# Three raw tiles of gated activations instead of four in the down stage of a decoder layer's MLP

## The chip, the cores and the metric

The kernel runs on one core of a Trainium2 chip. The metric is the device time of one execution in microseconds (us). TensorE does the matmuls, VectorE (DVE), ScalarE (ACT) and GpSimd (POOL) the elementwise work, and SyncE (SP) issues nearly all transfers between main memory and the on-chip memory, in the order of its queue.

## The reference

One layer of a hybrid decoder, float32, 2048 tokens of width 1024: a mixer of three head groups, then a gated MLP of 2688 channels, each with a residual. Only the MLP and the last norm matter here:

```python
h = rmsnorm(x, norm_ffn[l])
gate = causal_dwconv(h @ ffn_w_gate[l], ffn_conv_w[l], ffn_conv_b[l])   # width 3, along time
x = x + (jax.nn.gelu(gate) * (h @ ffn_w_val[l])) @ ffn_w_down[l]
...
return rmsnorm(x, norm_final)
```

## The kernel before, in words

Matrices are multiplied in split form: a float32 operand becomes a high half (a copy rounded to the matmul's type, made by ScalarE, line L100) and a low half (the rest, made by VectorE, L107), and `mm3` issues three matmuls for each product (L130 to L132). The helper `split` makes both halves; `load_w` loads a block of weights into a tile "wr" and splits it into "wh" and "wl".

The MLP goes over the tokens in two halves of 1024 (`hf` 0 and 1). In each half an *up stage* (`up`) goes over the NFF = 21 blocks of 128 channels; I call them channels 0 to 20. It makes the gate gr, its convolution and GELU ga, and the value v, from matmuls that all stand on line L993; its last steps are an add into gr (L1010), an add into v (L1013), another into gr (L1015), two convolution steps into ga (L1022), the GELU, the product v (L1025), and the store of v to main memory, `g_ffn[f]` (L1026). The tiles gr, ga and v of even channels, so of channel 20, lie in the pool f_up0, those of odd channels, so of channel 19, in f_up1.

The *down stage* (`down`) then multiplies g_ffn by w_down. It goes over groups of 2 to 4 row blocks of 128 tokens (3, 3 and 2 in the first half, 4 and 4 in the second). A group has 21 steps, one for each channel block: load a block of w_down, load the group's columns of g_ffn[f] into a raw tile "graw" (L1054), split that into "gh" and "gl", and issue 6 matmuls for each row block. In the first half a step is 18 matmuls with three row blocks and 12 with two. The next half's input is prepared beside the first half's down stage (tiles xt, L137 to L151, and the transposes).

```python
graw = gp.tile([P, 4 * P], F32, name="graw", bufs=4)[:, :n * P]
sync.dma_start(out=graw, in_=g_ffn[f][:, t0 * P:(t0 + n) * P])
g = [gp.tile([P, 4 * P], F32R, name=nm, bufs=3)[:, :n * P] for nm in ("gh", "gl")]
with tc.high_priority(offset=160):
    split(graw, g[0], g[1])
```

The up and down stages use the same memory, one after the other. In bytes of one partition from its start, the up stage leaves 8,192 free, then come channel 19's tiles in f_up1 (gr from 8,192), then channel 20's in f_up0: gr from 20,512, ga, v. The down stage's area f_g starts at 320 and holds graw, gh and gl in tiles of 2,048 bytes, with 4, 3 and 3 of them, so it ends at 320 + 10 x 2,048 = 20,800; its last tile is the gl of step 1. The area f_o with the norm's weights nfb and the residuals xr follows it. A down tile waits only for those up tiles whose bytes it takes (`reuse_waits="tile"`).

The order of instructions on each engine is made when the program is built, by a scheduler that places an instruction once it takes it to be ready, by priority; `tc.high_priority` moves an instruction forward. At run time each engine and the SP queue go through their own order and stop at an instruction whose inputs or tiles are not there.

Of the kernel before, what the change touches and what calls it, by code (L numbers as in the profile page):

```python
# [8 lines left out]
F32 = mybir.dt.float32  # L9
# [7 lines left out]
P = 128  # L17
# [26 lines left out]
def kernel(ctx: ExitStack, tc: tile.TileContext, x, norm_mix, w_in, hgrn_lower_bounds, hgrn_norm,  # L44
# [10 lines left out]
    def pool_at(stack, nbytes, name, bufs, **kw):  # L55

        stack.enter_context(tc.tile_pool(name="pad_" + name, bufs=1, **kw)).tile([P, nbytes // 4], F32, name="pad")
        return stack.enter_context(tc.tile_pool(name=name, bufs=bufs, **kw))
# [21 lines left out]
    def mm_bank():  # L80
        return bank("mm", 4)

    def aux_bank():
        return bank("aux", 2)

    def sc_bank():
        return bank("sc", 2)
# [16 lines left out]
    def split(raw, hi, lo, e_hi=act, e_lo=vec):  # L104

        copy(e_hi, hi, raw)
        e_lo.tensor_tensor(lo, raw, hi.bitcast(F32), op=ALU.subtract)  # L107

    def load_w(src, n1, n2, tag, tail=None, wpool=None, wcols=D):

        def part(pool_, dt, nm):
            return pool_.tile([P, wcols], dt, name=nm, tag=nm)[:, :n1 * n2].rearrange("p (a b) -> p a b", b=n2)
        hl = [part(wpool or wsp, F32R, "wh"), part(wpool or wsp, F32R, "wl")]
        raw = part(wraw, F32, "wr")
        if tail is None:
            sync.dma_start(out=raw, in_=src)
        else:
            m = src.shape[-1]
            sync.dma_start(out=raw[:, :, :m], in_=src)
            sync.dma_start(out=raw[:, :, m:], in_=tail)  # L120
        e_hi, e_lo, ahead = W_SPLIT[tag]
        with tc.high_priority(offset=ahead):
            split(raw, hl[0], hl[1], getattr(nc, e_hi), getattr(nc, e_lo))
        return hl
# [3 lines left out]
    def mm3(o, lhs, rhs, first, last):  # L128
        (lh, ll), (rh, rl) = lhs, rhs
        pe.matmul(o, lh, rh, start=first, stop=False)  # L130
        pe.matmul(o, lh, rl, start=False, stop=False)  # L131
        pe.matmul(o, ll, rh, start=False, stop=last)  # L132
# [90 lines left out]
    with ExitStack() as cx:  # L223
# [328 lines left out]
        for gi, group in enumerate((rows, frows)):  # L552
            n = sum(r[2] for r in group)
# [86 lines left out]
        for b in LEVELS[:5]:  # L640
            n = 64 // b
# [67 lines left out]
    with ExitStack() as cy:  # L709
# [319 lines left out]
        def down(hf, groups, gp, op, nfb, beside=()):  # L1029

            beside, t0, nst = list(beside), hf * TH // P, sum(1 for _ in groups) * NFF
            every, cnt = (nst // (len(beside) + 1) if beside else nst), 0
            for gi, n in enumerate(groups):
                banks = [[aux_bank(), sc_bank()] if t < 2 else [mm_bank(), mm_bank()] for t in range(n)]
                xr, ops = [], []

                def residuals():
                    for t in range(n):
                        two = n > 3 and t > 1
                        xr.append(xpool.tile([P, D], F32, name="xr2", tag="xt") if two else  # L1040
                                  op.tile([P, D], F32, name="xr", bufs=3))
                        r0 = (t0 + t) * P
                        sync.dma_start(out=xr[t], in_=x2_d[r0 // TB][r0 % TB:r0 % TB + P, :])

                def mms(t, h, f):
                    g, wd = ops[f]
                    mm3(banks[t][h], [a[:, t * P:(t + 1) * P] for a in g], [a[:, h, :] for a in wd],
                        f == 0, f == NFF - 1)

                late = 3 if (hf, gi) == (NH2 - 1, len(groups) - 1) else 2  # L1050
                for f in range(NFF):
                    wd = load_w(w_down[f * P:(f + 1) * P, :].rearrange("p (a c) -> p a c", a=2), 2, 512, "ffd")
                    graw = gp.tile([P, 4 * P], F32, name="graw", bufs=4)[:, :n * P]
                    sync.dma_start(out=graw, in_=g_ffn[f][:, t0 * P:(t0 + n) * P])  # L1054
                    g = [gp.tile([P, 4 * P], F32R, name=nm, bufs=3)[:, :n * P] for nm in ("gh", "gl")]
                    with tc.high_priority(offset=160):
                        split(graw, g[0], g[1])
                    ops.append((g, wd))
                    if f < NFF - late:
                        for t in range(n):  # L1060
                            for h in range(2):
                                mms(t, h, f)
                    if f == 8:
                        if gi == 0:
                            sync.dma_start(out=nfb, in_=norm_final.partition_broadcast(P))
                        residuals()
                    cnt += 1
                    if beside and cnt % every == 0:
                        beside.pop(0)()
                for t in range(n):  # L1070
                    y, sq = xr[t], op.tile([P, 2], F32, name="sq2", bufs=4)
                    for h in range(2):
                        for f in range(NFF - late, NFF):
                            mms(t, h, f)
                        ysl = y[:, h * 512:(h + 1) * 512]
                        vec.tensor_tensor(ysl, banks[t][h], ysl, op=ALU.add)
                        act.activation(junk_t(), ysl, AF.Square, accum_out=sq[:, h:h + 1])  # L1077
                    r = small.tile([P, 1], F32, name="rstd")
                    vec.tensor_tensor(r, sq[:, 0:1], sq[:, 1:2], op=ALU.add)
                    vec.tensor_scalar(r, r, 1.0 / D, EPS, op0=ALU.mult, op1=ALU.add)  # L1080
                    pool.tensor_tensor(r, r, half, op=ALU.pow)  # L1081
                    for h in range(2):
                        ysl = y[:, h * 512:(h + 1) * 512]
                        vec.scalar_tensor_tensor(ysl, ysl, r, nfb[:, h * 512:(h + 1) * 512], op0=ALU.mult, op1=ALU.mult)  # L1084
                        sync.dma_start(out=out[(t0 + t) * P:(t0 + t + 1) * P, h * 512:(h + 1) * 512], in_=ysl)
                t0 += n
            for st in beside:
                st()
# [5 lines left out]
        for hf in range(NH2):  # L1094
            with ExitStack() as cu:
                upools = [pool_at(cu, 8192, "f_up1", 1, reuse_waits="tile")]
                upools.insert(0, cu.enter_context(tc.tile_pool(name="f_up0", bufs=1, reuse_waits="tile")))
                up(hf, H, upools)
            with ExitStack() as cd_:
                gp = pool_at(cd_, 320, "f_g", 3, reuse_waits="tile")  # L1100
                op = cd_.enter_context(tc.tile_pool(name="f_o", bufs=1, reuse_waits="tile"))
                nfb = op.tile([P, D], F32, name="nfb")
                if hf + 1 < NH2:
                    H, steps = h_steps(hf + 1)
                    down(hf, (3, 3, 2), gp, op, nfb, steps)
                else:
                    down(hf, (4, 4), gp, op, nfb)
# [30 lines left out]
```

## Time and profile before

| | |
|---|---|
| median of 3 runs | 2282.15 us (2281.91 to 2282.93) |
| the profiled execution | 2290.03 us, with a span of 2288.3 us from first to last instruction |
| mean granted TensorE clock | 0.986 |
| first half: up stage, down stage | to 1381 us, to about 1630 us |
| second half: up stage, down stage | to 2036 us, to 2288 us |

Times in the rows are microseconds from the start of the profiled execution's span. A matmul's duration overlaps with the next one's, so distances between starts are used. The granted clock is the share of full speed at which TensorE was let run.

### The profile page before, as it was taken

To read this page: it belongs to the slowest core of one execution; us is meant where nothing else is said; L and a number is where in the kernel's file an instruction comes from. 1 tells how busy PE (TensorE), PEld (TensorE's weight loads), DVE (VectorE), ACT (ScalarE), POOL (GpSimd) and SP (SyncE) were. 2 spreads that over 40 slices of the span, in tenths; PEclk is the share of its full clock that TensorE was granted. 3 is DMA by queue.
4 is the path that set the end of the run, shared out by engine and by line. 5 is a ranking of instruction groups with operands and counts; after the bars stand their busy time and mean duration, and the time that the engine had idled before them with its cause. 6 is when DMAs were issued, how large, how long until landed. Compare 5 with 4: busy or idle time off the path is not lost. (4 is left out here: it accounts for less than half of the span.)

```text
span 2288.3 us, 31745 instructions
## 1 busy us (share of the span) xinstructions
PE 2195.2 (96%) x12310; PEld 1806.5 (79%) x12310; DVE 1591.1 (70%) x2212; ACT 998.1 (44%) x1375; POOL 350.3 (15%) x456
## 2 busy tenths in 40 slices
PE   7999999998999999999999998999999999989998
PEld 6887777776668789888888886888788888868886
DVE  7799998989577777766666664667766666643534
ACT  4453535342175375544444443556444444433322
POOL 2231432325242410000000000000000000000000
PEclk9999999999899999999999999999999999989999
DMA  7443322355146555622222236676522222254552
GB/s 260 130 148 115 136 80 61 93 174 176 28 143 222 164 167 170 205 85 83 83 83 83 84 101 199 191 240 227 175 83 83 83 83 83 83 172 150 173 181 88
DMA packets 272980, 307.27 MB, mean 134 GB/s; under 512 B 17203, under 2 KB 226110, under 8 KB 271294
## 3 DMA queue, kind: packets, MB, share of 16 engines
q1 hardware_dynamic: 272830, 305.26, 42.1%
q8 instruction: 96, 1.57, 0.3%
q14 instruction: 54, 0.44, 0.1%
HBM read 243.34 MB, written 61.87 MB: 133 GB/s over the span
## 5 line engine op out<-in xcount | busy, mean ns | idle before, releaser
L107 DVE TENSOR_TENSOR wl<-wr,wh 128x1024 fp32r<-128x1024 f32 (+2 forms) x289 | 328.3, 1139 | 130.8 <-ACT wh L100 125.9
L100 ACT ACTIVATE wh<-wr 128x1024 fp32r<-128x1024 f32 (+3 forms) x265 | 257.4, 974 | 251.4 <-PE mm L993 76.3
L130 PE MATMUL mm<-hTh,wh 128*128 128x512 f32 x576 | 235.0, 408 | 0.0
L132 PE MATMUL mm<-hTh,wl 128*128 128x512 f32 x576 | 232.6, 404 | 1.5 <-POOL wl L107 1.1
L131 PE MATMUL mm<-hTl,wh 128*128 128x512 f32 x576 | 233.1, 405 | 0.0
L398 POOL TENSOR_TENSOR qc<-Q,X 32x128 f32<-32x128 f32 x224 | 151.0, 674 | 247.2 <-ACT X L384 120.3
L107 DVE TENSOR_TENSOR gl<-graw,gh 128x384 fp32r<-128x384 f32 (+2 forms) x105 | 60.8, 583 | 183.3 <-ACT gh L100 173.9
L100 ACT ACTIVATE wh<-s 128x1024 fp32r<-128x1024 f32 x84 | 89.2, 1062 | 199.8 <-PE sc L993 173.2
L100 ACT ACTIVATE gh<-graw 128x384 fp32r<-128x384 f32 (+2 forms) x105 | 56.8, 544 | 240.1 <-PE mm L131 194.0
L131 PE MATMUL sc<-wl,oh 128*128 128x256 f32 x512 | 147.7, 289 | 2.2 <-DVE wl L107 2.2
L130 PE MATMUL sc<-wh,oh 128*128 128x256 f32 x512 | 147.2, 289 | 1.4 <-DVE xr L828 1.4
L132 PE MATMUL sc<-wh,ol 128*128 128x256 f32 x512 | 146.0, 285 | 0.0
L132 PEld LDWEIGHTS mm<-hTh,wl 128*128 128x128 f32 x576 | 109.1, 189 | 30.0 <-issue 4.3
L130 PEld LDWEIGHTS mm<-hTh,wh 128*128 128x128 f32 x576 | 109.2, 190 | 29.1 <-issue 7.1
L131 PEld LDWEIGHTS mm<-hTl,wh 128*128 128x128 f32 x576 | 109.1, 189 | 28.1 <-issue 7.3
L993 PE MATMUL mm<-t34h,wh 128*128 128x512 f32 x336 | 130.8, 389 | 0.0
L993 PE MATMUL mm<-t34l,wh 128*128 128x512 f32 x336 | 130.7, 389 | 0.0
L993 PE MATMUL mm<-t34h,wl 128*128 128x512 f32 x336 | 130.7, 389 | 0.0
L107 DVE TENSOR_TENSOR wl<-s,wh 128x1024 fp32r<-128x1024 f32 x84 | 102.5, 1221 | 9.5 <-ACT wh L100 9.5
L1022 DVE SCALAR_TENSOR_TENSOR ga<-gr,pcol,ga 128x1024 f32<-128x1024 f32 x84 | 107.7, 1282 | 0.1
L130 PE MATMUL aux<-wh,gh 128*128 128x512 f32 x210 | 83.6, 398 | 21.7 <-ACT gh L100 21.7
L131 PEld LDWEIGHTS sc<-wl,oh 128*128 128x128 f32 x512 | 98.2, 192 | 5.8 <-DVE wl L107 2.9
(302 smaller groups left out, 5696.0 us busy)
## 6 DMA issues: line engine op xcount, KB each, us to landing
wr<-in_ffn_w_down_dram SPq DMA_DIRECT2D x105, 512.0 KB
wr<-in_w_in_dram SPq DMA_DIRECT2D x80, 512.0 KB
wr<-in_ffn_w_gate_dram SPq DMA_DIRECT2D x42, 512.0 KB
wr<-in_ffn_w_val_dram SPq DMA_DIRECT2D x42, 512.0 KB
g_ffn<-v SPq DMA_DIRECT2D x42, 512.0 KB
wr<-in_w_out_dram SPq DMA_DIRECT2D x32, 512.0 KB
graw<-g_ffn SPq DMA_DIRECT2D x42, 256.0 KB
xt<-in_x_dram SPq DMA_DIRECT2D x16, 512.0 KB
```

The lines of the kernel that those rows point to most:

```text
L100: act.activation(o, i, AF.Copy)
L107: e_lo.tensor_tensor(lo, raw, hi.bitcast(F32), op=ALU.subtract)
L130: pe.matmul(o, lh, rh, start=first, stop=False)
L131: pe.matmul(o, lh, rl, start=False, stop=False)
L132: pe.matmul(o, ll, rh, start=False, stop=last)
L398: pool.tensor_tensor(qc[p_, h, :].rearrange("p (n s) -> p n s", s=lev), qo[p_, 2], xo[p_, 2], op=ALU.mult)
L993: pe.matmul(o, lhs[a], rhs[b], start=first and k == 0 and i == 0, stop=k == KH - 1 and i == 2, skip_group_check=True)
L1022: vec.scalar_tensor_tensor(ga, gr[:, k:k + TH], pc[f"fw{k}"][:, f:f + 1], ga, op0=ALU.mult, op1=ALU.add)
```

## The change

One number: the raw tiles of gated activations are three instead of four. f_g then ends at 320 + 9 x 2,048 = 18,752, below byte 20,512 where channel 20's gr starts, and f_o starts 2,048 bytes lower.

```diff
-                    graw = gp.tile([P, 4 * P], F32, name="graw", bufs=4)[:, :n * P]
+                    graw = gp.tile([P, 4 * P], F32, name="graw", bufs=3)[:, :n * P]
```

TensorE's order is the same as before. SP's changes at the start of the first down stage; below, g_ffn_97 to g_ffn_117 are the blocks of channels 0 to 20, x_d is the residual's stream in main memory, and "wr" a block of w_down. Before:

```order
L1026 DMA g_ffn_116<-v 128x1024
L116 DMA wr<-in_ffn_w_down_dram 128x1024 x4
L1026 DMA g_ffn_117<-v 128x1024
L1054 DMA graw<-g_ffn_97 128x384
L1054 DMA graw<-g_ffn_98 128x384
L1054 DMA graw<-g_ffn_99 128x384
L1054 DMA graw<-g_ffn_100 128x384
L1065 DMA nfb<-in_norm_final_dram 128x1024
```

And now, from the same store of channel 19:

```order
L1026 DMA g_ffn_116<-v 128x1024
L1054 DMA graw<-g_ffn_97 128x384
L1054 DMA graw<-g_ffn_98 128x384
L1054 DMA graw<-g_ffn_99 128x384
L116 DMA wr<-in_ffn_w_down_dram 128x1024
L1054 DMA graw<-g_ffn_100 128x384
L116 DMA wr<-in_ffn_w_down_dram 128x1024
L1054 DMA graw<-g_ffn_101 128x384
L1054 DMA graw<-g_ffn_102 128x384
L116 DMA wr<-in_ffn_w_down_dram 128x1024 x2
L1026 DMA g_ffn_117<-v 128x1024
```

The first loads of graw moved from behind the store of channel 20 to right behind that of channel 19, ahead of four loads of w_down. At the start of the second down stage SP's order changes in the same way, except that one load of w_down stands between the second and the third graw.

On VectorE, in the last channel of the first up stage, before:

```order
L107 TENSOR_TENSOR wl<-wr,wh 128x512
L1010 TENSOR_TENSOR gr<-aux,gr 128x512
L107 TENSOR_TENSOR wl<-wr,wh 128x1024
L1013 TENSOR_TENSOR v<-mm,v 128x512
L1015 TENSOR_TENSOR gr<-sc,gr 128x512
L107 TENSOR_TENSOR wl<-wr,wh 128x1024
L1022 SCALAR_TENSOR_TENSOR ga<-gr,pcol_400,ga 128x1024 x2
L107 TENSOR_TENSOR wl<-wr,wh 128x1024
L1025 TENSOR_TENSOR v<-ga,v 128x1024
L107 TENSOR_TENSOR gl<-graw,gh 128x384 x4
```

And now:

```order
L107 TENSOR_TENSOR wl<-wr,wh 128x512
L107 TENSOR_TENSOR gl<-graw,gh 128x384
L1010 TENSOR_TENSOR gr<-aux,gr 128x512
L107 TENSOR_TENSOR wl<-wr,wh 128x1024
L107 TENSOR_TENSOR gl<-graw,gh 128x384 x2
L1013 TENSOR_TENSOR v<-mm,v 128x512
L1015 TENSOR_TENSOR gr<-sc,gr 128x512
L107 TENSOR_TENSOR wl<-wr,wh 128x1024
L1022 SCALAR_TENSOR_TENSOR ga<-gr,pcol_400,ga 128x1024 x2
L107 TENSOR_TENSOR wl<-wr,wh 128x1024
L1025 TENSOR_TENSOR v<-ga,v 128x1024
L107 TENSOR_TENSOR gl<-graw,gh 128x384
```

Three low halves "gl" moved from behind the product v of channel 20 to places between its adds. ScalarE's high halves moved with them. In the second half the third stands behind the add into v (L1013).

The third place is SP's queue at the start of the two-block group, around the stores of the group before it ("out"), as a piece of the difference:

```order
 L1054 DMA graw<-g_ffn_100 128x256
-L116 DMA wr<-in_ffn_w_down_dram 128x1024
-L1054 DMA graw<-g_ffn_101 128x256
 L116 DMA wr<-in_ffn_w_down_dram 128x1024
 L1085 DMA out_dram<-xr 128x512 x2
 L1043 DMA xr<-x_d_119 128x1024
 L1085 DMA out_dram<-xr 128x512
-L116 DMA wr<-in_ffn_w_down_dram 128x1024 x2
+L116 DMA wr<-in_ffn_w_down_dram 128x1024
+L1054 DMA graw<-g_ffn_101 128x256
+L116 DMA wr<-in_ffn_w_down_dram 128x1024
```

The load for step 4 (g_ffn_101) moved from ahead of three stores to behind them. Elsewhere in the down stages a load of graw stands one step later than before in the same way.

## Rows read from the trace of the kernel before

**Rows 1.** The page, busy time, share of the span and instructions of an engine.

```profile
PE 2195.2 (96%) x12310; PEld 1806.5 (79%) x12310; DVE 1591.1 (70%) x2212; ACT 998.1 (44%) x1375; POOL 350.3 (15%) x456
```

**Rows 2.** TensorE's waits, 1375 to 1720 us, then 2035 to the end.

```profile
PE aux L130 <- ACT gh L100: 10.5, 1, 10.5
PE sc L993 <- DVE wl L107: 1.2, 1, 1.2
...
PE aux L130 <- ACT gh L100: 11.3, 1, 11.3
```

**Rows 3.** Busy time by stretch around the first seam, with clock and data share.

```profile
core 0: us, PE busy (x) PEld busy (x) DVE busy (x) ACT busy (x) POOL busy (x), PEclk, DMA share, GB/s
1360.00:1380.00 20.00, 20.00 (x90) 16.57 (x89) 13.69 (x16) 11.27 (x16) 1.46 (x4) 1.00 0.39 131
1380.00:1390.00 10.00, 1.16 (x6) 0.62 (x4) 5.41 (x5) 3.05 (x4) 0.00 (x0) 0.83 0.62 188
1390.00:1400.00 10.00, 8.37 (x26) 6.74 (x27) 2.36 (x5) 2.94 (x5) 0.00 (x0) 0.66 0.89 293
1400.00:1410.00 10.00, 10.00 (x45) 8.26 (x45) 4.50 (x5) 2.96 (x4) 0.00 (x0) 1.00 0.62 189
```

**Rows 4.** The SP queue in order of time: start, duration, instruction, count.

```profile
1361.61 4.05 SPq L145 DMA_DIRECT2D xt<-x_d  x2
1366.55 0.32 SPq L1026 DMA_DIRECT2D g_ffn<-v  x1
...
1385.47 0.33 SPq L1026 DMA_DIRECT2D g_ffn<-v  x1
1385.85 0.42 SPq L1054 DMA_DIRECT2D graw<-g_ffn  x1
```

**Rows 5.** First seam, order of time; in brackets the idle time before.

```profile
1380.77 0.39 PE L993 MATMUL mm<-t34h,wl 128*128 128x512 f32 x1
...
1391.06 1.46 ACT L100 ACTIVATE gh<-graw 128x384 fp32r<-128x384 f32 x3 [6.87 <-DMA graw<-g_ffn]
...
1391.63 0.79 PE L130 MATMUL aux<-wh,gh 128*128 128x512 f32 x1 [10.47 <-ACT gh L100]
...
1396.84 0.40 PE L130 MATMUL mm<-wh,gh 128*128 128x512 f32 x1
...
1401.62 0.39 PE L130 MATMUL mm<-wh,gh 128*128 128x512 f32 x1
```

**Rows 6.** Second seam, order of time.

```profile
2036.06 0.39 PE L993 MATMUL mm<-t34h,wl 128*128 128x512 f32 x1
...
2041.21 2.44 SPq L1054 DMA_DIRECT2D graw<-g_ffn  x4
...
2047.04 0.63 ACT L100 ACTIVATE gh<-graw 128x512 fp32r<-128x512 f32 x1 [7.50 <-DMA graw<-g_ffn]
...
2047.73 0.79 PE L130 MATMUL aux<-wh,gh 128*128 128x512 f32 x1 [11.27 <-ACT gh L100]
...
2052.37 0.39 PE L132 MATMUL sc<-wh,gl 128*128 128x512 f32 x1
```

**Rows 7.** VectorE and TensorE in the last channel before the first seam.

```profile
1375.76 0.69 DVE L1013 TENSOR_TENSOR v<-mm,v 128x512 f32<-128x512 f32 x1 [0.62 <-PE mm L993]
...
1378.28 0.39 PE L993 MATMUL mm<-t34h,wh 128*128 128x512 f32 x1
...
1383.01 1.22 DVE L107 TENSOR_TENSOR wl<-wr,wh 128x1024 fp32r<-128x1024 f32 x1
```

**Rows 8.** Start of the two-block group, order of time.

```profile
1578.25 0.42 DVE L107 TENSOR_TENSOR gl<-graw,gh 128x256 fp32r<-128x256 f32 x1
...
1581.06 0.41 DVE L107 TENSOR_TENSOR gl<-graw,gh 128x256 fp32r<-128x256 f32 x1
...
1581.60 0.38 SPq L1054 DMA_DIRECT2D graw<-g_ffn  x1
...
1585.68 0.42 ACT L100 ACTIVATE gh<-graw 128x256 fp32r<-128x256 f32 x1 [0.74 <-DMA graw<-g_ffn]
1585.85 0.39 PE L132 MATMUL aux<-wh,gl 128*128 128x512 f32 x1
```

## The prediction

> **What bounds the kernel now.** I read the page first: TensorE is busy for 96% of the span [rows 1]. So only the other 4% can be had, and the question is where they lie and whether the change touches one of them. TensorE's waits in the two down stages answer it [rows 2]: one wait of 10.5 and one of 11.3 us, each at the start of a down stage, both for a high half "gh" of the gated activations, which ScalarE makes; the next longest is 1.2 us. The busy times by stretch show the first hole from the clock's side [rows 3]: from 1380 to 1390 us TensorE works 1.16 us of 10, in the next 10 us its granted clock is 0.66, and from 1400 us on the clock is full and there is no gap.
>
> Then the rows around that hole, in order of time. The SP queue stores channel 19 at 1366.55, channel 20 at 1385.47, and only behind that store, at 1385.85, issues the first load "graw" [rows 4]. TensorE's last matmul of the up stage had started at 1380.77; ScalarE splits the load at 1391.06, and TensorE goes on at 1391.63 [rows 5]. So the hole is a store that waits for the last gate's arithmetic, then a load queued behind it that needs nothing from it (it reads what channel 0 stored), then 5.2 us of landing (1385.85 to 1391.06), then the split. The second hole is alike, with 5.8 us of landing (2041.21 to 2047.04) [rows 6].
>
> **The change part by part.** No instruction is added or removed; some move, as the orders above show. Three loads now stand directly behind the store of channel 19, about 19 us earlier in the first down stage, and on VectorE the first three low halves stand between the steps of channel 20's gate instead of behind it. The code says why: with four tiles the area f_g ran to byte 20,800, past the start (20,512) of the last channel's gr; with three it ends at 18,752.
>
> *Removed, first hole.* At full clock a matmul of the down stage starts every (1401.62 - 1396.84) / 21 = 0.2276 us [rows 5]. The next one could have started at 1380.77 + 0.23 = 1381.00 and started at 1391.63: 10.63 us. The 12 matmuls from there to 1396.84 took 5.21 us instead of 12 x 0.2276 = 2.73, the clock being at the lower of its two levels (1.2 of 2.4 GHz) after the hole: 2.48 us.
>
> *Removed, second hole.* From 2036.06 + 0.23 = 2036.29 to 2047.73: 11.44 us. The 11 matmuls from there to 2052.37 took 4.64 us instead of 2.50: 2.14 us [rows 6]. The four terms make **26.7 us**.
>
> *What is late next.* Step k of the first down stage (18 matmuls, 4.10 us) would start at 1381.00 + 4.10 k and needs block k of w_down split. Of the first three blocks the last split began at 1383.01 and took 1.22 us [rows 7], for a step that starts at 1389.2. Blocks 3 to 5 were asked for ahead of the store of 1385.47, as the queue's order shows, and block 3 is needed at 1393.3. Nothing is late; I cost this at zero.
>
> *Added ahead of the up stage's end.* Three splits, about 0.5 us each on ScalarE (1.46 for three [rows 5]) and much the same on VectorE. The latter now stand ahead of the add into v (L1013), which ran at 1375.76 and must have read its bank before TensorE's product of 1378.28 [rows 7]. VectorE worked 13.69 of the 20 us from 1360 to 1380 [rows 3], so 1.5 us have room; what matters is that the loads have landed. They go out from about 1366.9, some 0.6 us apart (four took 2.44 us [rows 6]), the third at 1368.1, and its split must end by about 1377.5: some 8 us to land. A first load behind a 512 KB store took 5.2 and 5.8 us, the same neighbour as here. I take zero, with bounds of 0 and 2 us. In the second down stage the third load stands behind a w_down load, but its split also stands behind the add, so the cover is larger.
>
> *The steady down stages.* With one raw tile less a load is issued one step later. The steps take 4.1 us (three row blocks, 42 steps), 5.5 (four, 42) and 2.7 (two, 21); three tiles cover three steps, 12.3, 16.4 and 8.2 us, against at most 5.8 us of landing and about 1.1 us of splits. The start of the two-block group is tightest. There step 4's tile was split at 1581.06, long before TensorE wanted it at 1585.85; step 5's load went out at 1581.60 and was split from 1585.68, 4.1 us later [rows 8]. Now step 4's load must wait for the low half of step 1, which ran at 1578.25 for 0.42 us: it goes out at 1578.7 and lands at 1582.8. On VectorE it stands behind two more instructions of about 1.2 us (a w_down split is 1.22 [rows 7]), so it is ready at about 1585.1, 0.7 us before its use. Below: no cost. Above: one more such split ahead of it makes 0.8 us late at this and the two other later group starts, 2.4 us. I take 1.0, nearer the low end, since only one of the three has short steps.
>
> *Sum.* 26.7 - 1.0 = 25.7 us off. The profiled execution took 2290.03 us, its span 2288.3; the median of the runs is 2282.15, 7.9 us less. I take the 25.7 off the median unscaled: **2256.5 us** (and a span of 2262.6 in a profile). If all the 7.9 us of profiling lay inside the two holes, the gain would be 17.8 and the time 2264.4; that is a bound for the range.
>
> **Rivals.**
>
> *Partly given back at the seam.* The loads land late behind the store, hold VectorE in its order, and the add into v with it. Each us beyond 8 of landing is a us of TensorE there; landings of 10 to 13 us give back 2 to 5 us a seam, 4 to 10 in both: 2260 to 2267 us. For it: the store and a load of xt issued by 1365.66 [rows 4] are in flight at the time. Against it: 5.2 us of landing was measured in a stretch that moved 188 to 293 GB/s, and the new place moves 131 [rows 3].
>
> *The early loads help little.* The splits wait for the last channel after all, so that they run behind its store (1385.47) with their data there: TensorE restarts at about 1386, each hole shrinks by 5.6 us, 2271 us. Against it: in the new order they stand ahead of channel 20's adds, so they cannot wait for what follows these.
>
> *The gain is given back later, no change.* The first stage could be paced by its data: 0.52 MB of w_down and 0.20 MB of graw in each 4.10 us is 176 GB/s. If that were the limit, TensorE would reach the same point at the same time: 2282 us. Against it: from 1400 to 1410 us 189 GB/s were moved at a share of 0.62 with TensorE full [rows 3].
>
> *Slower: three raw tiles starve the down stages.* A load is issued only when the low half three steps before is done. If landing and splits together exceed three steps, each step waits a third of the excess. In the two-block group that is (L + 1.1 - 8.2) / 3 x 21 = 7 x (L - 7.1) us for a landing of L; three-block groups join at L = 11.2. To eat 26.7 us and 4.6 more, L must be about 11.3 us; at 11.5 it costs 31 + 4 = 35 us, so 2290 us. For it: ScalarE waited for the load in the row of step 5 [rows 8]. Against it: 4.1 us there is a third of what it takes. The Trainium skill, Perfetto Trace Analysis, section Identifying the Most-Contended Engine, says that consistent bubbles on the engine that should be saturated can mean too little memory for the next tile, and names the buffer count; by it one tile less is the wrong direction and would show as a small gap at every step. With four tiles this trace shows no such gap, and no run here yet shows three.
>
> **How the numbers follow.** Forecast (2252.5 to 2260): 0.78. Partly given back (2260 to 2267): 0.10. Early loads help little: 0.04. No change: 0.04. Slower: 0.04. The low end is 29.7 us off: the 1.0 not paid and 3 us of small waits such as the 1.2 of [rows 2] shortened by the new order. The high end takes in the given-back case and 2264.4: 2252.5 to 2267 leaves out little more than 1 in 10. A measurement of this kernel can tell about 0.2%, 4.6 us, from no change. Faster by more than that: 0.78 + 0.10 + 0.04 = 0.92; within it 0.04; slower 0.04.
>
> **What would show it.** Right: the first graw load is issued near 1367 us, right behind the store of channel 19; the down stages list no wait of TensorE above 2 us; the granted clock stays at 1.00 from 1370 to 1410 us and around 2040; the first matmul of line 130 into aux follows the up stage's last within 0.5 us. Wrong: TensorE waiting for L1013 near 1378 (seam), many waits for gh or gl inside a group (starved), or two long waits still there. What would break the prediction most easily is loads that land much later beside the store of channel 19 than they did behind that of channel 20.

## The result, and the profile after

The changed kernel took 2255.94 us (median of 4 runs, 2254.81 to 2259.39), the kernel before in the same comparison 2282.54 us (4 runs). The ratio is 0.9881, with a 95% interval of 0.9862 to 0.9900: faster by 26.6 us, where 25.7 was forecast. The time of 2255.94 us lies 0.6 us from the forecast 2256.5 and inside its range. The profiled execution took 2259.39 us with a span of 2257.4, and the mean granted clock was 0.994 instead of 0.986.

TensorE's busy time is 8.1 us less with the same number of instructions (its row on the page after, beside [rows 1]). A matmul at the lower clock counts as busy, so a part of what was to be gained (4.6 us by the forecast's two terms) never showed as idle time. The other 3.4 us lie ahead of the first seam (1322.75 us busy there before, 1319.36 now).

```profile
PE 2187.1 (97%) x12310; PEld 1802.6 (80%) x12310; DVE 1590.5 (70%) x2212; ACT 998.1 (44%) x1375; POOL 350.8 (16%) x456
```

TensorE's waits in the changed kernel, 1345 to 1700 us and then 2000 to 2260 us (waiting line, what it waited for, total, count, longest). Both waits for gh of 10.5 and 11.3 us [rows 2] are gone, and nothing above 1.5 us is in their place:

```profile
PE sc L993 <- DVE wl L107: 1.5, 1, 1.5
PE mm L910 <- DVE xt L151: 1.2, 1, 1.2
...
PE mm L130 <- DVE xr L1076: 0.9, 1, 0.9
```

Its SP queue at the first seam (start, duration, instruction). The three loads stand directly behind the store of channel 19, and 18.6 us ahead of the store of channel 20, behind which they stood in [rows 4]:

```profile
1361.80 0.32 SPq L1026 DMA_DIRECT2D g_ffn<-v  x1
1362.16 2.09 SPq L1054 DMA_DIRECT2D graw<-g_ffn  x3
...
1380.72 0.33 SPq L1026 DMA_DIRECT2D g_ffn<-v  x1
```

The same seam on ScalarE, VectorE and TensorE, each in order of time. The first load, issued at 1362.16, was split from 1366.53, so it landed in at most 4.37 us. The three low halves run ahead of the add into v (L1013) at 1371.23. The last matmul of the up stage starts at 1376.01 and the first of the down stage at 1376.24, one matmul later, where [rows 5] has 10.86 us between these two:

```profile
1366.53 0.53 ACT L100 ACTIVATE gh<-graw 128x384 fp32r<-128x384 f32 x1
1369.02 0.92 ACT L100 ACTIVATE gh<-graw 128x384 fp32r<-128x384 f32 x2
...
1367.69 0.55 DVE L107 TENSOR_TENSOR gl<-graw,gh 128x384 fp32r<-128x384 f32 x1
1370.30 1.02 DVE L107 TENSOR_TENSOR gl<-graw,gh 128x384 fp32r<-128x384 f32 x2
1371.23 0.69 DVE L1013 TENSOR_TENSOR v<-mm,v 128x512 f32<-128x512 f32 x1
...
1376.01 0.39 PE L993 MATMUL mm<-t34h,wl 128*128 128x512 f32 x1
1376.24 0.39 PE L130 MATMUL aux<-wh,gh 128*128 128x512 f32 x1
```

Busy time by stretch there, to be set beside [rows 3]: TensorE is full and the granted clock 1.00 in every stretch. The transfers now are heavier before the seam (190 GB/s where there were 131):

```profile
core 0: us, PE busy (x) PEld busy (x) DVE busy (x) ACT busy (x) POOL busy (x), PEclk, DMA share, GB/s
1355.00:1375.00 20.00, 20.00 (x90) 16.58 (x89) 15.02 (x19) 12.62 (x19) 1.46 (x4) 1.00 0.58 190
1375.00:1385.00 10.00, 10.00 (x46) 8.29 (x45) 7.46 (x8) 5.36 (x8) 0.00 (x0) 1.00 0.59 197
1385.00:1395.00 10.00, 10.00 (x46) 8.29 (x45) 5.07 (x6) 3.85 (x5) 0.00 (x0) 1.00 0.95 332
```

At the second seam, beside [rows 6], the first load goes out at 2004.83, is split 4.66 us later, and the matmuls run on from 2018.69 to 2018.92:

```profile
2004.83 1.31 SPq L1054 DMA_DIRECT2D graw<-g_ffn  x2
...
2009.49 0.63 ACT L100 ACTIVATE gh<-graw 128x512 fp32r<-128x512 f32 x1 [0.31 <-DMA graw<-g_ffn]
...
2018.69 0.39 PE L993 MATMUL mm<-t34h,wl 128*128 128x512 f32 x1
2018.92 0.39 PE L130 MATMUL aux<-wh,gh 128*128 128x512 f32 x1
```

**Where the time came from.** The two spans differ by 30.9 us, more than the runs do, so I cut them at events that both have: the start of the last matmul of the up stage (L993) at the first seam, the same at the second, and the span's end. Each of the last two columns below holds one down stage, its seam included (the middle one also the second half's up stage); I call these two numbers of a kernel its distances. The span is read to 0.1 us, so the last column is good to that.

| | start to first seam | first to second seam | second seam to end |
|---|---|---|---|
| before | 1380.77 | 655.29 | 252.24 |
| after | 1376.01 | 642.68 | 238.71 |
| difference | -4.76 | -12.61 | -13.53 |
| forecast | 0 | -13.11, part of the 1.0 off | -13.58, part of the 1.0 off |

The last two columns give 26.14 us. The 4.76 us of the first lie in code whose order on TensorE is the same, and over all the kernels profiled below, whatever their edit, this stretch took 1371.2 to 1381.8 us; I count it as the difference between executions. Where the stage is the same, the distances repeat within 1.1 us (the middle column, 641.56 to 642.68) and 0.3 us (the last), so the experiments are read by them and the medians stand beside them.

### The profile page after: what moved, and what is told of

Same layout as the page of the kernel before. It is cut to its first block, busy times and chain, and to the rows that moved or that the text cites. A ratio compares the mean times of both kernels' runs of the same rounds, so it can differ in the third digit from the quotient of the medians.

```text
span 2257.4 us, 31761 instructions
## 1 busy us (share of the span) xinstructions
PE 2187.1 (97%) x12310; PEld 1802.6 (80%) x12310; DVE 1590.5 (70%) x2212; ACT 998.1 (44%) x1375; POOL 350.8 (16%) x456
## 4 chain that ended last, share of the span: by engine, by line
PE 58%; DVE 5%; DMA 2%; ACT 2%; issue 2%; POOL 1%; SPq 0%; DVEq 0%; POOLq 0%; ACTq 0%
PE mm L993 20%; PE sc L993 10%; PE aux L993 5%; PE sc L131 3%; PE sc L130 3%; PE sc L132 3%; PE mm L130 2%; PE mm L131 2%; PE mm L132 2%; PE aux L132 2%; PE aux L131 2%; PE aux L130 2%; DMA xt<-x_d 1%; DMA oa<-o_ac_d 1%; PE mm L910 1%
## 5 line engine op out<-in xcount | busy, mean ns | idle before, releaser
L993 PE MATMUL mm<-t34h,wh 128*128 128x512 f32 x336 | 131.0, 390 | 0.0
L993 PE MATMUL mm<-t34l,wh 128*128 128x512 f32 x336 | 130.9, 389 | 0.0
L993 PE MATMUL mm<-t34h,wl 128*128 128x512 f32 x336 | 130.8, 389 | 0.0
L130 PEld LDWEIGHTS sc<-wh,oh 128*128 128x128 f32 x512 | 97.7, 191 | 6.1 <-DVE xr L828 3.6
```

What stands on the lines that cost most here:

```text
L993: pe.matmul(o, lhs[a], rhs[b], start=first and k == 0 and i == 0, stop=k == KH - 1 and i == 2, skip_group_check=True)
```

## The experiments

Theory: the number of raw tiles does nothing by itself; the area's end does. Where it reaches into the tiles of channel 20, the program is built with all early loads behind the store of channel 20, and that order costs the time. Rivals: the count of tiles matters by itself (fewer loads in flight, less traffic); only the run-time wait of the one overlapping tile matters; one of the two seams carries the gain; three tiles already cost something in the steady stages.

**Four tiles, area clear.** The up stage's tiles of channel 19, and with them those of channel 20, begin 288 bytes higher, so that four raw tiles end below gr of channel 20.

```diff
-                upools = [pool_at(cu, 8192, "f_up1", 1, reuse_waits="tile")]
+                upools = [pool_at(cu, 8480, "f_up1", 1, reuse_waits="tile")]
```

> Four raw tiles as before, but the up stage's free bytes are 8,480 instead of 8,192, so that channel 20's gr starts at 20,800, just where the down stage's area with four tiles ends. Theory 1 (what costs is that the area reaches into the last channel's tiles, which puts the first loads behind that channel's store; the number of raw tiles does not matter): both holes are gone as with three tiles, 2255 to 2258 us, no wait of TensorE above 2 us at the seams. Theory 2 (the gain is that of fewer raw tiles: less data in flight, another order within the groups): near the kernel before, 2278 to 2284 us.

Measured: 2257.38 us, ratio 0.9884 (0.9869 to 0.9898); distances 642.00 and 238.66; TensorE's longest wait from 1345 to 1700 us is 1.2 us. Four tiles are as good as three where they are clear.

**The changed kernel again**, in the same comparison.

> The changed kernel once more, for comparison on the same chip. All theories: 2255 to 2257 us. If a fourth raw tile is worth the 0.5 to 1 us that the forecast charged for its loss, the run with four tiles and a clear area is faster than this one by that much; more than 3 us would say that the loss of the tile costs more than the forecast has.

Measured: 2257.74 us, ratio 0.9888 (0.9872 to 0.9903); distances 642.15 and 238.58. So 0.4 us lie between three and four tiles.

**Three tiles, area over.** The changed kernel, with the area moved up by a larger pad (the second argument of `pool_at`, the free bytes ahead of the area) until its end (20,544) reaches 32 bytes into gr of channel 20.

```diff
-                    graw = gp.tile([P, 4 * P], F32, name="graw", bufs=4)[:, :n * P]
+                    graw = gp.tile([P, 4 * P], F32, name="graw", bufs=3)[:, :n * P]
-                gp = pool_at(cd_, 320, "f_g", 3, reuse_waits="tile")
+                gp = pool_at(cd_, 2112, "f_g", 3, reuse_waits="tile")
```

> Three raw tiles, but the pad ahead of the area is 2,112 bytes instead of 320, so that the area ends at 20,544, 32 bytes past the start of channel 20's gr. Theory 1: as the kernel before, two holes of 10 to 12 us, 2280 to 2284 us. Theory 2: as the changed kernel, 2255 to 2258 us. If only the run-time wait of the overlapping tile counted (the low half of step 1, free when channel 20's convolution has read gr) and not the place of the loads in the queue, the holes would be near 1 us and the time about 2258.

Measured: 2282.30 us, ratio 0.9998 (0.9988 to 1.0008): three tiles and no gain at all. TensorE's waits, 1345 to 1700 us and 1990 to 2260 us, are those of before:

```profile
PE aux L130 <- ACT gh L100: 10.5, 1, 10.5
...
PE aux L130 <- ACT gh L100: 11.7, 1, 11.7
```

and its SP queue has four loads of w_down, the store of channel 20 and only then the three loads, though the raw tiles share no byte with channel 20:

```profile
1364.54 11.85 SPq L116 DMA_DIRECT2D wr<-in_ffn_w_down_dram  x4
1377.27 0.33 SPq L1026 DMA_DIRECT2D g_ffn<-v  x1
1377.68 2.02 SPq L1054 DMA_DIRECT2D graw<-g_ffn  x3
```

So it is not a wait of the overlapping tile at run time; the loads were placed behind the store when the program was built. Why the scheduler holds back all the loads for one tile that overlaps isn't seen in a trace.

**Three tiles, area ending exactly at gr's first byte** (pad 2080), and **32 bytes clear of it** (pad 2048); otherwise the edit just shown.

> Three raw tiles with a pad of 2,080 bytes: the area ends at 20,512, on the very byte where channel 20's gr starts, 32 bytes less than the run with a pad of 2,112. Theory 1: no hole, 2255 to 2258 us. If the size of the gap or the place of nfb and xr (which follow the area) counted, something between that and 2282.

> Three raw tiles with a pad of 2,048 bytes: the area ends at 20,480, 32 bytes below channel 20's gr, and all tiles start at multiples of 64 bytes, as in the kernel before and the changed one; in the run with a pad of 2,080 they started 32 bytes beside such multiples, and every matmul of the down stages took 0.2334 us instead of 0.2268. Theory A (that shift is what cost 12 us there; the edge itself is sharp): 2255 to 2258 us, matmuls 0.2268 us apart. Theory B (an area that ends next to the last channel's tiles is slower for another reason): 2265 us or more.

Measured: 2268.20 us, ratio 0.9933 (0.9913 to 0.9952), and 2260.05 us, 0.9910 (0.9895 to 0.9925). Neither has a hole: with 2080 the matmuls run on from 1378.66 to 1378.89. So the edge lies between an end at 20,512 and one at 20,544, at the first byte of gr. But the distances are 647.31 and 244.43 with 2080, and 643.82 and 240.63 with 2048, 10.3 and 3.1 us longer in sum than those of the changed kernel. That was a new effect, and the runs at pads 352 and 384 below follow it.

**One seam at a time.** Three tiles in the first half alone, then in the second alone.

```diff
+                    graw = gp.tile([P, 4 * P], F32, name="graw", bufs=3 if hf == 0 else 4)[:, :n * P]
...
+                    graw = gp.tile([P, 4 * P], F32, name="graw", bufs=4 if hf == 0 else 3)[:, :n * P]
```

> Three raw tiles in the first down stage, four in the second. The forecast's terms, one seam at a time: 10.63 + 2.48 less some tenths for the steady stage are saved at the first seam, and the second hole of 11.4 us stays: 2282.5 - 12.6 = 2269.9 us, within 1.5. Theory 2 would give no sharp split.

> Four raw tiles in the first down stage, three in the second: the first hole stays, the second goes with 11.44 + 2.14 us: 2282.5 - 13.5 = 2269.0 us, within 1.5. The two single savings should add up to that of the whole change, 26.5 us; if the sum is off by more than 2 us, the two seams are not independent or something else of the change counts.

Measured: 2270.53 us, ratio 0.9945 (0.9928 to 0.9962), and 2266.67 us, 0.9925 (0.9910 to 0.9941). What is left in each, the first half changed (1990 to 2260 us) and then the second (1345 to 1700 us):

```profile
PE aux L130 <- ACT gh L100: 11.4, 1, 11.4
```

```profile
PE aux L130 <- ACT gh L100: 10.5, 1, 10.5
```

The distances are 641.56 and 251.96, and 655.02 and 238.58: the first seam is worth 655.29 - 641.56 = 13.7 us and the second 252.24 - 238.58 = 13.7 us. The savings by the medians (15.7 and 19.6 us below a kernel before that took 2286.26 us in that comparison) make 35.3, where 26.5 within 2 us was expected. The kernel before was slow in that comparison, 2286.26 against 2282.54 in that of the result, and this counts in both savings; with 2282.54 they are 12.0 and 15.9. So I take the distances: the second seam of the one kernel (251.96) and the first of the other (655.02) are within 0.3 us of the kernel before.

**Two raw tiles**, to find where a starved down stage begins.

> Two raw tiles. The area stays clear of the last channel. Theory 1 with the forecast's formula: two tiles cover two steps, 8.2 and 10.9 us in the groups of three and four blocks, which is more than landing and splits (5.8 + 1.1), and 5.5 us in the two-block group, where 4.1 + 1.1 just fits: 2256 to 2262 us, the excess in the two-block group. If landing there is 5.8 us, (6.9 - 5.5) / 2 x 21 = 15 us more, 2271 us. Theory 2 (fewer tiles are faster): below 2255 us. The rival that few tiles starve the down stages: small waits for gh or gl at most steps, above 2275 us.

Measured: 2260.49 us, ratio 0.9904 (0.9887 to 0.9921); distances 645.59 and 238.65, so 2.9 us lost against the changed kernel, all in the first down stage. Busy time from the first to the last matmul start of the two-block group, with two tiles and in the changed kernel:

```profile
1561.39:1624.64 63.25, 61.52 (x268) 47.97 (x267) 48.26 (x71) 38.08 (x62) 2.17 (x4) 1.00 0.75 242
```

```profile
1555.73:1615.55 59.82, 59.53 (x269) 48.61 (x267) 47.34 (x70) 37.70 (x62) 2.16 (x4) 1.00 0.78 253
```

The group takes 3.4 us longer, and the group before it as long as in the changed kernel (91.71 and 91.74 us), so the whole loss lies in the two-block group. TensorE's list there has 0.5 us of waits for gh and 0.6 us for xt; what the rest waits for it doesn't say. With two tiles ScalarE waits for the load inside the group, in its order of time:

```profile
1571.82 0.42 ACT L100 ACTIVATE gh<-graw 128x256 fp32r<-128x256 f32 x1 [0.95 <-DMA graw<-g_ffn]
```

So the starving rival is real in the group with the shortest steps, but with one tile less than the change has, and it is worth at most 3.4 us.

**Four tiles overlapping, loads issued by GpSimd.** The area stays as before, but the loads are no longer in the queue of the stores.

```diff
-                    sync.dma_start(out=graw, in_=g_ffn[f][:, t0 * P:(t0 + n) * P])
+                    pool.dma_start(out=graw, in_=g_ffn[f][:, t0 * P:(t0 + n) * P])
```

> Four raw tiles with the overlap, as before, but the loads of graw are issued by GpSimd's queue instead of SP's. Theory 1a (the hole is the store of channel 20 ahead of the loads in SP's queue): in GpSimd's queue they stand behind only the last channel's copy of carry, so they go out near 1380 instead of 1385.9 and land before the gate's end; the splits still stand behind the product v on VectorE (end 1385.4), so TensorE restarts near 1386: each hole shrinks from 10.5 and 11.3 to 5 or 6 us, some 11 us in all, 2268 to 2274 us, if GpSimd's issue costs nothing elsewhere. Theory 1b (the loads land no earlier, since the data share is what sets their landing): holes as before, 2280 us or more.

Measured: 2276.95 us, ratio 0.9965 (0.9949 to 0.9982); waits of 4.3 and 3.8 us are left. First seam on GpSimd, ScalarE and TensorE:

```profile
1372.39 0.19 POOL L1016 COPY carry_f<-gr 128x2 f32<-128x2 f32 x1 [8.59 <-DVE gr L1015]
1373.13 2.38 POOL L1054 DMA_DIRECT2D graw<-g_ffn  x4 [0.55 <-issue]
...
1377.93 0.52 ACT L100 ACTIVATE gh<-graw 128x384 fp32r<-128x384 f32 x1 [0.67 <-DMA graw<-g_ffn]
...
1373.86 0.39 PE L993 MATMUL mm<-t34h,wl 128*128 128x512 f32 x1
1378.51 0.50 PE L130 MATMUL aux<-wh,gh 128*128 128x512 f32 x1 [4.27 <-ACT gh L100]
```

The first load leaves 0.73 us before the last matmul of the up stage; in [rows 4, 5] it left 5.08 us after it. That is 5.81 us earlier, and it lands in 4.80 us instead of 5.21: together 6.22 us, and the hole shrank from 10.47 to 4.27, by 6.20. So when the load goes out and lands sets the hole, to a few hundredths of a microsecond. It was still late because GpSimd's own queue stands at the copy of channel 20's carry, which waits for L1015. The distances shrink by only 4.84 and 1.55 us, and the time lies above the 2268 to 2274 us of theory 1a. In the first down stage some 2 us are lost again later, 1.2 of them in a second wait for xt. In the second the kernel's end is 5 us longer: 13.8 us from the start of the last matmul to the span's end, 8.7 in the changed kernel. The trace shows what stands there. At the end of the program (line L1133) every engine runs a drain; here are GpSimd's and SP's (count, then shortest, median and longest in ns, then first and last start), and below them GpSimd's in the changed kernel:

```profile
L1133 POOLq DRAIN  x3: 40/102/9241, 2265.0 to 2274.7; - x3
L1133 SPq DRAIN  x3: 7/7/7, 2269.2 to 2274.5; - x3
```

```profile
L1133 POOLq DRAIN  x3: 34/78/642, 2252.4 to 2257.1; - x3
```

GpSimd's first drain takes 9.24 us, from 2264.99 to 2274.23, where it took 0.64. SP has seen the last outputs off by 2269.3, so the last 5 us are GpSimd's drain alone. What it waits for isn't in the trace.

**The place of the halves.** Pads of 2080 and 2048 moved not only the area's end but the start bytes of graw, gh and gl. Pads of 352 and 384 shift all tiles by 32 and 64 bytes with the end far below 20,512; a third kernel puts a tile of 32 bytes between graw and the halves at pad 352, so that graw is shifted by 32 and the halves by 64. The order of instructions on every engine is that of the changed kernel in these three and at pad 2048.

```diff
-                gp = pool_at(cd_, 320, "f_g", 3, reuse_waits="tile")
+                gp = pool_at(cd_, 352, "f_g", 3, reuse_waits="tile")
...
+                    if (gi, f) == (0, 0):
+                        gp.tile([P, 8], F32, name="shift", bufs=1)
```

> The changed kernel with a pad of 352 instead of 320 bytes: the area is 1,728 bytes clear of channel 20's tiles, but graw, gh, gl, nfb and xr start 32 bytes beside multiples of 64. The order of instructions is that of the changed kernel. Theory A (the shift costs 6.6 ns a matmul): 2,016 matmuls of the down stages x 6.6 ns = 13.3 us, 2267 to 2271 us. Theory B: 2256 us.

> As the run with a pad of 352, and a 32-byte tile between the raw tiles and the halves, so that only graw is shifted by 32 bytes and gh, gl, nfb and xr start at multiples of 64 again. If the cost lies in TensorE's read of the halves as its stationary operand: 2256 us, matmuls 0.2268 us apart. If it lies in the loads or the splits' reads: 2262 us or more, with waits for gh and gl.

> The changed kernel with a pad of 384 instead of 320 bytes, so that graw, gh, gl, nfb and xr all start 64 bytes past a multiple of 512, where the changed kernel has gh and gl on multiples of 512; the halves stand on the same bytes as in the run in which only graw was to be shifted (64 past a multiple of 512 there too, which I had overlooked), but graw is at a multiple of 64 now. If the place of the halves alone sets the matmuls' pace: 0.2333 us between matmuls and 2265 to 2270 us. If the 32-byte shift of graw did it: 0.2268 us and 2255 to 2258 us; something between, as in the run with a pad of 2,048 (halves 192 past a multiple of 512, 0.2289 us), would leave open which bytes count.

Measured: pad 352 2268.59 us, ratio 0.9945 (0.9930 to 0.9961); with the small tile 2266.19, 0.9929 (0.9912 to 0.9946); pad 384 2265.74, 0.9929 (0.9912 to 0.9946). None has a hole, but the distances of the last are 647.37 and 244.50. The kernel with the small tile answers neither branch of its expectation: it has the time of the second without its waits, since its halves were shifted too. The loss is in every matmul of the down stage. First and last of 27 that follow each other without a gap, at pad 384:

```profile
2059.66 0.39 PE L131 MATMUL aux<-wl,gh 128*128 128x512 f32 x1
...
2065.73 0.39 PE L130 MATMUL sc<-wh,gh 128*128 128x512 f32 x1
```

and 27 of the changed kernel:

```profile
2059.72 0.39 PE L130 MATMUL mm<-wh,gh 128*128 128x512 f32 x1
...
2065.61 0.39 PE L132 MATMUL mm<-wh,gl 128*128 128x512 f32 x1
```

That is 6.07 / 26 = 0.2335 us from start to start, against 5.89 / 26 = 0.2265. Over the whole second down stage (1,008 matmuls) the first and the last start lie 235.93 us apart at pad 384 and 229.77 us in the changed kernel, 6.2 us, with the granted clock at 1.00 in both. The kernel with the small tile, whose graw is shifted by 32 and whose halves by 64 bytes, has 235.94 us. So graw at 32 or at 64 makes no difference, and TensorE doesn't read graw. Of the tiles that it reads in this stage these edits move only the halves. No run moved graw alone, and none gh or gl alone. The chip isn't the cause either: one and the same ran pad 2080 at 0.2333 us and the two kernels with one half changed at 0.2267.

## Why the prediction was right

*What bounds the kernel, and the mechanism.* Right. The holes came from the order in SP's queue: three tiles, area over, has the count of the change and the time of before; four tiles, area clear, has the count of before and the time of the change; the loads issued by GpSimd shrink the hole by as much as they leave and land earlier.

*Removed, both seams.* Forecast 10.63 + 2.48 and 11.44 + 2.14, 26.7 us. Measured by the distances: 12.61 and 13.53 us in the changed kernel, 13.7 for each seam alone (the two kernels with one half changed), where the terms give 13.11 and 13.58. The two terms for the lower clock can be read by themselves. From the first to the last matmul of the second down stage the kernel before took 231.91 us and the changed one 229.77, so 2.14 us, as forecast. From the first matmul of the first down stage to the 379th they took 90.24 and 87.75, so 2.49 where 2.48 was forecast.

*Landing and the add L1013.* I allowed 8 us for the early loads to land and costed the splits ahead of L1013 at zero, bounds 0 and 2. The first load of each seam landed in at most 4.4 and 4.7 us, against 5.2 and 5.8 behind the store of channel 20. So the size holds, but the argument for it doesn't: the 131 GB/s of [rows 3] were read where these loads weren't yet. While the first one was under way, as much was moved as in its old place (the last two numbers are the data share and GB/s; first the changed kernel, then the one before):

```profile
1362.16:1366.53 4.37, 4.37 (x21) 3.60 (x20) 2.14 (x4) 2.87 (x5) 1.09 (x2) 1.00 0.95 324
```

```profile
1385.85:1391.06 5.21, 0.00 (x0) 0.00 (x0) 0.00 (x0) 0.00 (x1) 0.00 (x0) 0.56 0.98 312
```

That the landing was no longer there was luck as far as this argument goes; what the forecast had right is the room of 8 us. L1013 started 4.78 us before the last L993, in [rows 5, 7] 5.01 us before it: 0.23 us later, and TensorE didn't wait for it. Zero holds.

*What is late next.* I costed the blocks of w_down at zero. In the first down stage TensorE's list has one wait for them, 0.3 us, and the kernel before has the same. Zero holds.

*The steady down stages.* Forecast 1.0 us (0 to 2.4). By the accounting it is 26.7 - 26.14 = 0.55 us, and four clear tiles against three give 0.36 us of medians; neither is more than the difference between executions. Closer is the two-block group from its first to its last matmul: 59.82 and 59.67 us in the two runs of the changed kernel, 59.63 with four clear tiles and 59.61 before. So the third tile costs 0 to 0.2 us there: the bounds hold, and 1.0 was too much. At the start of the two-block group, which I called the tightest, the order of time has step 4's load, its low half on VectorE, and TensorE's first use of that half:

```profile
1560.85 0.33 SPq L1054 DMA_DIRECT2D graw<-g_ffn  x1
...
1566.49 0.42 DVE L107 TENSOR_TENSOR gl<-graw,gh 128x256 fp32r<-128x256 f32 x1
...
1568.03 0.39 PE L132 MATMUL aux<-wh,gl 128*128 128x512 f32 x1
```

It was ready 1568.03 - 1566.91 = 1.1 us before its use; I had worked out 0.7.

*The time.* Taking the whole 25.7 us off the median was right; the 7.9 us between the profiled execution and the median didn't lie in the holes (the bound of 2264.4 falls). That forecast and result agree to 0.6 us is partly luck: the interval allows a gain of 22.8 to 31.5 us, and the changed kernel's two medians differ by 1.8. The profiled span was 2257.4 us, not 2262.6; 4.76 of the 5.2 us lie ahead of the first seam, where no term of the forecast lies.

*The rivals.* Partly given back and "the early loads help little" fall by the matmul at 1376.24, no change by the clock and the full TensorE at up to 332 GB/s. Starving falls for three tiles, since TensorE's longest wait for gh or gl in the down stages is 0.4 us, which the kernel before has too; the run with two tiles shows its size one step further on. The Trainium skill, Perfetto Trace Analysis, section Optimization Strategy (the prediction names the section ahead of it), says that a gap that repeats for a stretch on the engine that should be saturated can mean too little memory for the next tile, and names the buffer count. The two holes here didn't repeat, and closed with one buffer less: the runs show them to be a matter of where the buffers lie. The 3.4 us lost in one group with two tiles agree with the rule in kind. What I hadn't seen is that moving the area, rather than shortening it, would have cost up to 10.7 us by the distances (pads 352, 384 and 2080); the change leaves the halves where they aren't slowed, since one tile of 2,048 bytes less moves them by four times 512 bytes.

What stays open: why the scheduler places all loads late for one overlapping tile, and which bits of the halves' start byte matter.

## What to carry to other kernels

Where a stage reuses the memory of the one before, compare the end of its area with the start of the last tiles still in use, byte by byte: here 32 bytes over or 32 bytes clear decide 22 us (2282.30 against 2260.05 us), and 26 us where the halves aren't slowed. Where a load that needs nothing stands behind a waiting store in the queue at a seam, look for the order in which the program was built: here a buffer less or 288 bytes of shift undid it, and another queue did so in part (waits of 4.3 and 3.8 us were left). When tiles are shifted, read the distance between TensorE's matmuls afterwards: the hole may close and the pace get worse.

## What the runs showed of the hardware that I had not expected

The start byte of the halves, which TensorE loads as 128 x 128 blocks of 512 bytes per row, sets the pace of its matmuls. The byte numbers in this document count from the start of the shared area, which the program puts at byte 191,680 of a partition, so the halves of before start at multiples of 512 bytes. By the remainder of the halves' start divided by 512, the down stage's matmuls start 0.2267 to 0.2268 us apart at 0 (before, after, four tiles clear) and 256 (three tiles, area over), 0.2289 at 192 (pad 2048), and 0.2333 to 0.2334 at 32 (352), 64 (384, and 352 with the small tile) and 224 (2080), all at a granted clock of 1.00. In the second down stage that is 2.0 us at 192 (231.80 us from first to last matmul against 229.77) and 6.2 us at 64; by the distances 10.5 us for both down stages at pad 384. That 192 lies between has no explanation here. The recorded weight loads last as long in the slow kernels (188 ns at pad 384 as in the changed kernel), so the trace doesn't show in which part of a matmul the time goes.

GpSimd takes 0.54 us to issue a load (the median of the 105 loads of graw), SP 0.32, and the drain at the program's end then takes GpSimd 9.24 us instead of 0.64:

```profile
L1054 POOL DMA_DIRECT2D graw<-g_ffn x105: 536/538/755, 1373.1 to 2224.7; - x105
```

```profile
L1054 SPq DMA_DIRECT2D graw<-g_ffn x105: 319/320/847, 1362.2 to 2217.4; - x105
```
